# Decoder layer with a product-key mixture of experts: second tile's expert selection moved behind the first one-hots, gates evicted key by key, all second norms closed on VectorE

## The chip, the cores and the metric

The kernel runs on one core of a Trainium2 chip. The metric is the time of one execution on the device in microseconds (us); runs are compared by their medians. Engine names: PE is TensorE (matmuls), DVE is VectorE, ACT is ScalarE, POOL is GpSimd, SP is SyncE, which issues most DMAs.

## The reference

One decoder layer over 512 tokens of width 1024. A token mixer (sliding-window attention beside a gated linear recurrence) is followed by a layer norm, and then by a mixture of 16,384 experts, each a single neuron, chosen by product keys. The part that matters here is that mixture and the norm behind it:

```
q = (ht @ peer_w_q).reshape(T, 8, 2, 128)
s1, s2 = q[:, :, 0] @ keys_1.T, q[:, :, 1] @ keys_2.T
v1, i1 = top_k(s1, 16);  v2, i2 = top_k(s2, 16)
sc, ci = top_k(v1[..., :, None] + v2[..., None, :], 16)
experts = 128 * i1[ci // 16] + i2[ci % 16]
gates = softmax(sc)
out = sum over the 128 experts e of a token:  gate * gelu(h . u[e]) * v[e]
h = layer_norm(ALPHA * h + out)
```

## The kernel before

The 512 tokens are four tiles of 128. Three of them (tiles 1, 2 and 3, in this order) are "dense": the kernel computes the activation of all 16,384 experts for every token and multiplies it by a gate that is zero for an expert not chosen. Tile 0 is done last by gathering the rows of its chosen experts from memory.

After the mixer the work goes through these stages.

- **Queries and scores.** `query(i)` (16 of them, lines 755 to 766) multiplies a block of the query weights with all tokens; `scores(i)` (768 to 777) multiplies the result with the keys, and `top16` (737 to 751) takes, on DVE, the 16 best of 128 keys for each of four tiles.
- **Selection.** `experts(t)` (796 to 870) is a generator that DVE works off in steps for one tile: for each half of the eight heads it adds up candidate scores (`cand`, lines 807 to 813), takes the 16 best (`top16` into `esc` and `pos`), and turns positions into key numbers by comparisons and sums over 128 x 1024 tables (`ge`, `pr`, lines 821 to 847; there is one buffer of each). A step ends at each `yield`; the first half of a head set gives 4 yields, the second 6, and then the softmax and the key numbers `ex` follow.
- **One-hots and gates.** For a dense tile `gate_prep` (878) transposes the key numbers and gates on PE (line 881) and DVE copies them out (`eT`, `gT`, lines 883 and 886). In 48 steps of 8 tokens (16 steps for a tile), `onehots` (898) builds one-hot rows of both key numbers on DVE (lines 910, 917 and 918, with a part on ACT in line 916), and `gate_mm` (923) multiplies them on PE into a PSUM tile `psg` of 8 tokens x 128 keys. That tile is evicted: keys 60 to 127 go to a staging tile `gst` on ACT (line 936) and from there to memory; keys 0 to 59 meet the activations that are kept in `act`: those whose activation is already there are multiplied on DVE (line 939), the rest is copied on ACT (line 941).
- **Activations.** `u_block` (255 to 283) makes the activations of 128 experts for the 384 dense tokens: a 512 KB block of `uT` is loaded, split into two f16 parts on ACT (line 202) and DVE (line 203, `wl`), and multiplied in 24 matmuls of 384 columns. These blocks are what PE does between the gate matmuls.
- **Second matmul and gathers.** From about 605 us PE alternates the remaining `u_block`s with `vblock`s (1051), while DVE and POOL do the gathered tile.
- **Second norm.** `finish(t)` (1140 to 1162) adds the residual, takes the mean and the inverse deviation with `layer_stats` and `rsqrt` on DVE, normalises and stores.

The order on each engine is not written out by hand. The program is recorded in the order of the Python code, and a list scheduler puts each engine's instructions in a static order; `tc.issue_after(last[0].ins)` (line 1003) holds the selection steps behind the newest one-hots. In the loop over queries (981 to 987) the selections of tiles 1 and 2 both advance by one step in each of the four iterations 8 to 11, which covers the first half of the heads of either tile. The rest of tile 1's selection follows in lines 990 to 992, interleaved with `u_block`s; the rest of tile 2's is worked off by `steps(gen, ...)` (line 1004) during tile 1's 16 one-hot steps, two steps each in the first four and one each after that.

In the eviction, `o2` is the PSUM tile as (token, key), `GST[0]` and `W[0]` have the key ahead of the token, and `part` turns the destination, so that the innermost index of both sides is the key: PSUM is read word after word, and `gst` and `act` are read and written with a distance between neighbours (16 and 384 words).

Of the kernel before, what the change touches and what calls it, by code (L numbers as in the profile page):

```python
# [9 lines left out]
F32 = mybir.dt.float32  # L10
# [4 lines left out]
AF = mybir.ActivationFunctionType  # L15
OP = mybir.AluOpType
AX = mybir.AxisListType.X

P = 128
S = 512  # L20
D = 1024
NT = 4
# [22 lines left out]
NW = 60  # L45
# [93 lines left out]
def program(tc, nc, a, out, dbg=None, stop=None):  # L139
    ctx = ExitStack()  # L140
    with ctx:
        _program(ctx, tc, nc, a, out, dbg or {}, stop)


def _program(ctx, tc, nc, a, out, dbg, stop):
    V, A, G, T = nc.vector, nc.scalar, nc.gpsimd, nc.tensor
# [19 lines left out]
    def mk(pool, shape, dt, tag, bufs):  # L166
        uid[0] += 1
        return pool.tile(shape, dt, name=f"{tag}_{uid[0]}", tag=tag, bufs=bufs)
# [58 lines left out]
    def layer_stats(pool, src, tag):  # L227
        st = mk(pool, [P, 2, 6], F32, tag + "st", 2)
        for i in range(2):
            V.bn_stats(st[:, i], src[:, i * 512:(i + 1) * 512])  # L230
        mv = mk(pool, [P, 2], F32, tag + "mv", 2)
        V.bn_aggr(mv, st)
        ve = mk(pool, [P, 1], F32, tag + "ve", 2)
        V.tensor_scalar(ve, mv[:, 1:2], EPS, None, op0=OP.add)
        return mv, rsqrt(pool, ve, tag)
# [3 lines left out]
    def raw4():  # L239
        return mk(rp, [P, 1024], F32, "raw", RAW_BUFS)  # L240
# [383 lines left out]
    for c in range(4):  # L624
        rnn_ssq(c, sqr[c])
    V.tensor_reduce(ssq.rearrange("p t k -> p (t k)"), ssp[:, :8 * NT].rearrange("p (a g) -> p a g", g=4), axis=AX,
                    op=OP.add)
# [11 lines left out]
    for c in range(DC):  # L639
        r = raw4()  # L640
# [69 lines left out]
    pp = ctx.enter_context(tc.tile_pool(name="pp", bufs=1))  # L710
# [44 lines left out]
    def query(i):  # L755
        r = raw4().rearrange("p (c e) -> p c e", c=DC)
        nc.sync.dma_start(r, a["w_q"][i])
        wh, wl = whl()
        split(r, wh, wl, int((i + 1) * Q_POOL) > int(i * Q_POOL))
        o = bank()  # L760
        for sl in (slice(T0, S), slice(0, T0)) if i == 0 else (slice(0, S),):
            for c in range(DC):
                mm3(o[:, sl], wh[:, c], wl[:, c], hh[:, c, sl], hl[:, c, sl], c, c == 0, c == DC - 1)
        qt = mk(gp, [P, S], F32, "k2", K2_BUFS)
        A.activation(qt, o, AF.Copy, scale=1.0 / WS)
        QT[i] = qt

    def scores(i):
        hd, side = divmod(i, 2)
        qt = QT.pop(i)  # L770
        o = bank()
        for t in range(NT):
            T.matmul(o[:, t * P:(t + 1) * P], qt[:, t * P:(t + 1) * P], keys[:, side], start=True, stop=True)
        sc = mk(gp, [P, NT, NKEY], F32, "k2", K2_BUFS)
        A.activation(sc, o.rearrange("p (t k) -> p t k", t=NT), AF.Copy)
        top16([(VV[t][:, hd, side], II[t][:, hd, side], sc[:, t]) for t in TORDER],
              lambda i, src, w=mk(gp, [P, NT, NKEY], F32, "k2", K2_BUFS): w[:, i])
# [7 lines left out]
    first = {}  # L785
# [90 lines left out]
    NB = 8  # L876
# [44 lines left out]
    GST = {}  # L921

    def gate_mm(col0, ob, oh, ol):
        o2 = mk(PB["g"][0], [P, NB, P], F32, "psg", PB["g"][1])
        for t in range(NB):
            q = (slice(None), t // R, slice(None), t % R)
            T.matmul(o2[:, t], ob[q], oh[q], start=True, stop=False)
            T.matmul(o2[:, t], ob[q], ol[q], start=False, stop=True)
        ch, q = divmod(col0, TCH)
        if q == 0:  # L930
            GST[0] = mk(gp, [P, NKEY - NW, TCH], F32, "gst", 2)

        def part(ap):
            return ap.rearrange("p e r -> p r e")

        A.activation(part(GST[0][:, :, q:q + NB]), o2[:, :, NW:], AF.Copy)
        na = min(nact[0], NW)
        wc = W[0][:, :, col0:col0 + NB]
        V.tensor_tensor(part(wc[:, :na]), part(wc[:, :na]), o2[:, :, :na], op=OP.mult)
        if na < NW:  # L940
            A.activation(part(wc[:, na:]), o2[:, :, na:NW], AF.Copy)
        ncol[0] = col0 + NB
        if q == TCH - NB:
            i = max(i for i in range(NQ) if cut[i] <= ch)
            nc.sync.dma_start(gscr[i][:, :, ch - cut[i]].rearrange("g p e t -> p g e t"),
                              GST[0].rearrange("p (g e) t -> p g e t", e=GE))
# [30 lines left out]
    order = TORDER  # L977
# [3 lines left out]
    for i in range(2 * HEADS):  # L981
        query(i)
        if i:
            scores(i - 1)
        if HEADS <= i < HEADS + YH:
            for t in first:
                next(first[t])
    scores(2 * HEADS - 1)
    banks(2, 2)
    while not next(first[order[0]], 1):  # L990
# [8 lines left out]
    for s in range(NS):  # L999
        i, k = divmod(s, SPT)  # L1000
        if k == 0:
            gen = first[order[1]] if i == 0 else experts(order[2]) if i == 1 else iter(())
        with tc.issue_after(last[0].ins):
            steps(gen, 99 if k == SPT - 4 else 2 if k < 4 else 1)
        if k == SPT - 1 and i + 1 < ND:
            gate_prep(order[i + 1])
        nxt = onehots(order[(s + 1) // SPT], (s + 1) % SPT * NB) if s + 1 < NS else None
        if nu[0] < NW - RES:
            u_block()
        gate_mm(s * NB, *pend)  # L1010
        pend = nxt
# [11 lines left out]
    def rows(*offs, scale=None):  # L1023
        rr = []
        for off in offs:
            r = mk(dg[0], [P, D], F32, "gr", GR_BUFS)
            nc.sync.dma_start(r, rowb(off, D))
            if scale is not None:
                A.activation(r, r, AF.Copy, scale=scale)
            rr.append(r)  # L1030
        return rr
# [37 lines left out]
    for b in range(NKEY):  # L1069
# [3 lines left out]
        g, k = divmod(b - NW, GE)  # L1073
# [21 lines left out]
        if b >= NW:  # L1095
            wc = w.rearrange("p (c t) -> p c t", t=TCH)
# [6 lines left out]
        if b == NKEY - NY:  # L1103
            l2g, l2b = rows(R_L2G, R_L2B)
            l1 = rows(R_L1G, R_L1B, scale=ALPHA)
            res = {}
            for t in range(NG, NT):
                y = raw4()
# [31 lines left out]
    def finish(t):  # L1140
        if t < NG:
            y = gacc[t]
            V.tensor_tensor(y, ah[t], gacc[t], op=OP.add)
        else:
            y = res[t]
            for hf in range(2):
                sl = slice(hf * 512, hf * 512 + 512)
                V.scalar_tensor_tensor(y[:, sl], acc[t - NG][hf], 1.0 / GS, y[:, sl], op0=OP.mult, op1=OP.add)
        mv, ri = layer_stats(pp, y, "ln2")
        if t == NT - 1:  # L1150
            for hf in range(2):
                sl = slice(hf * 512, hf * 512 + 512)
                V.scalar_tensor_tensor(y[:, sl], y[:, sl], mv[:, 0:1], l2g[:, sl], op0=OP.subtract, op1=OP.mult)
                V.scalar_tensor_tensor(y[:, sl], y[:, sl], ri, l2b[:, sl], op0=OP.mult, op1=OP.add)
                (nc.sync, nc.scalar)[hf].dma_start(out[t * P:(t + 1) * P, sl], y[:, sl])
            return
        nm = mk(pp, [P, 1], F32, "ln2nm", 2)
        V.scalar_tensor_tensor(nm, mv[:, 0:1], -1.0, ri, op0=OP.mult, op1=OP.mult)
        A.activation(y, y, AF.Identity, scale=ri, bias=nm)
        V.tensor_tensor(y, y, l2g, op=OP.mult)  # L1160
        V.tensor_tensor(y, y, l2b, op=OP.add)
        nc.sync.dma_start(out[t * P:(t + 1) * P], y)

    for t in range(NT - 1):
        finish(t)
    with tc.high_priority():
        finish(NT - 1)
# [15 lines left out]
```

## Time and profile before

| | us |
|---|---|
| median of 3 runs (1374.76 to 1376.82) | 1375.07 |
| the profiled execution, its own time | 1375.56 |
| its span, first to last instruction | 1373.8 |
| PE busy | 1327.5 (97%) |
| DVE busy | 1192.3 (87%) |
| ACT busy | 678.6 (49%) |
| POOL busy | 394.8 (29%) |

The span is shorter than the execution's own time by what lies before the first and behind the last instruction. The shares are averages over stages with different limits, so they have to be read stage by stage; PE's matmuls overlap each other, and a busy PE is not PE at its peak.

### The profile page before, as it was taken

The numbers are of one execution on the slowest core, as the hardware profiler recorded it, in microseconds if no ns is written. First come the engines' busy times: TensorE is split into PE (matmuls) and PEld (weight loads), VectorE is DVE, ScalarE is ACT, GpSimd is POOL, SyncE is SP. The second block draws the span as 40 slices with busy tenths as digits, with TensorE's granted clock in tenths as the row PEclk, the third lists the DMA queues.
The fourth block names the chain that finished last, engine by engine and source line by source line (L and its number), as shares of the span: only waits on it lengthen the run. The fifth ranks groups of instructions, "written<-read, shape, count | busy, mean of one in ns | idle before, by whom it ended". The sixth has DMA issues, their size and how long they took to land.

```text
span 1373.8 us, 21409 instructions
## 1 busy us (share of the span) xinstructions
PE 1327.5 (97%) x7601; PEld 721.3 (53%) x7601; DVE 1192.3 (87%) x2555; ACT 678.6 (49%) x1155; POOL 394.8 (29%) x300
## 2 busy tenths in 40 slices
PE   8999999998999989999999999999999999999996
PEld 3554555554666656655555555555555554444442
DVE  7956766899899998989898888888898889988887
ACT  5755165434798877765433333333333333333341
POOL 0103412300000000000654545445454555545400
PEclk9998999999999999999999999999999999999998
DMA  8103053223465564665999999999999999998851
GB/s 308 64 16 123 3 176 118 93 74 123 129 167 158 145 173 135 167 228 183 394 408 396 356 355 369 364 365 366 367 361 358 351 346 365 354 330 306 305 207 74
DMA packets 142859, 332.49 MB, mean 242 GB/s; under 512 B 62880, under 2 KB 63392, under 8 KB 142752
## 3 DMA queue, kind: packets, MB, share of 16 engines
q1 hardware_dynamic: 105168, 195.59, 42.4%
q0 software_dynamic: 36864, 134.23, 26.4%
q8 instruction: 59, 0.97, 0.3%
q10 hardware_dynamic: 720, 1.31, 0.3%
q14 instruction: 48, 0.39, 0.1%
HBM read 313.53 MB, written 17.56 MB: 241 GB/s over the span
## 4 chain that ended last, share of the span: by engine, by line
PE 76%; DVE 18%; ACT 2%; issue 2%; DMA 2%; POOL 0%; DVEq 0%; SPq 0%; ACTq 0%; POOLq 0%
PE psv L1056 22%; PE psv L1058 11%; PE psu L208 8%; PE psu L206 8%; PE psu L207 8%; PE psv L206 3%; PE psv L207 3%; PE psv L208 3%; DVE wl L203 3%; DVE oab L910 2%; PE psv L475 2%; DVE k L917 1%; PE psv L661 1%; PE psv L662 1%; PE psv L663 1%
## 5 line engine op out<-in xcount | busy, mean ns | idle before, releaser
L715 POOL DMA_INDIRECT gr<-u,ei x128 | 162.7, 1271 | 524.8 <-ACT act L278 369.6
L206 PE MATMUL psu<-hh,wh 128*128 128x384 f16 (+2 forms) x816 | 265.4, 326 | 7.1 <-ACT wh L202 3.0
L208 PE MATMUL psu<-hh,wl 128*128 128x384 f16 (+1 forms) x816 | 265.7, 326 | 5.1 <-DVE wl L203 5.1
L207 PE MATMUL psu<-hl,wh 128*128 128x384 f16 (+1 forms) x816 | 265.6, 326 | 0.0
L202 ACT ACTIVATE wh<-raw 128x1024 f16<-128x1024 f32 (+1 forms) x141 | 147.8, 1048 | 193.7 <-PE psu L207 150.1
L1056 PEld LDWEIGHTS <-w_h 128*128 128x128 f16 x1536 | 150.3, 98 | 173.5
L203 DVE SCALAR_TENSOR_TENSOR wl<-raw,wh 128x1024 f16<-128x1024 f32 (+1 forms) x141 | 171.3, 1215 | 66.1 <-ACT wh L202 65.8
L715 POOL DMA_INDIRECT gr<-v,ei x128 | 170.6, 1333 | 164.7 <-DVE gacc L967 144.4
L1099 ACT ACTIVATE w_h<-act 128x384 f16<-128x384 f32 x128 | 66.1, 521 | 255.7 <-PE psv L1056 254.3
L206 PEld LDWEIGHTS <-wh 128*128 128x128 f16 x1232 | 121.4, 99 | 102.6 <-ACT wh L202 9.4
L1056 PE MATMUL psv<-vl,w_h 128*128 128x512 f16 x582 | 173.4, 379 | 0.0
L1058 PE MATMUL psv<-vh,w_l 128*128 128x512 f16 x582 | 173.4, 379 | 0.0
L208 PEld LDWEIGHTS <-wl 128*128 128x128 f16 x1232 | 121.2, 98 | 99.0 <-DVE wl L203 9.1
L1056 PE MATMUL psv<-vh,w_h 128*128 128x512 f16 x582 | 171.6, 379 | 0.0
L207 PEld LDWEIGHTS <-wh 128*128 128x128 f16 x1232 | 121.4, 99 | 94.3 <-issue 7.9
L967 DVE SCALAR_TENSOR_TENSOR gacc<-gr,gact,gacc 128x1024 f32<-128x1024 f32 x127 | 162.4, 1279 | 0.7
L957 DVE SCALAR_TENSOR_TENSOR gr<-gr,ah 128x1024 f32<-128x1024 f32 x128 | 154.0, 1216 | 1.4 <-DMA gr<-u,ei 1.3
L1094 DVE TENSOR_TENSOR vl<-rv,vh 128x1024 f16<-128x1024 f32 x97 | 118.1, 1218 | 7.6 <-ACT vh L1093 7.6
L1058 PEld LDWEIGHTS <-w_l 128*128 128x128 f16 x768 | 75.1, 98 | 90.6
L208 PE MATMUL psv<-hh,wl 128*128 128x384 f16 (+2 forms) x352 | 119.8, 342 | 1.9 <-DVE wl L203 1.9
L206 PE MATMUL psv<-hh,wh 128*128 128x384 f16 (+2 forms) x352 | 119.8, 342 | 1.5 <-ACT act L278 0.8
L207 PE MATMUL psv<-hl,wh 128*128 128x384 f16 (+2 forms) x352 | 119.9, 342 | 0.0
(264 smaller groups left out, 2050.3 us busy)
## 6 DMA issues: line engine op xcount, KB each, us to landing
raw<-uT SPq DMA_DIRECT2D x128, 512.0 KB, 4.8
rv<-v SPq DMA_DIRECT2D x98, 512.0 KB, 6.8
raw<-v SPq DMA_DIRECT2D x30, 512.0 KB, 7.1
gs<-gst SPq DMA_DIRECT2D x24, 544.0 KB, 4.2
gsb<-gs SPq DMA_DIRECT2D x34, 384.0 KB, 8.5
raw<-w_q SPq DMA_DIRECT2D x16, 512.0 KB, 4.2
raw<-w_in SPq DMA_DIRECT2D x13, 512.0 KB, 4.8
raw<-w_out SPq DMA_DIRECT2D x8, 512.0 KB, 4.3
```

The costliest lines, as they stand in the source:

```text
L202: A.activation(hi, raw, AF.Copy, scale=WS)
L203: V.scalar_tensor_tensor(lo, raw, WS, hi, op0=OP.mult, op1=OP.subtract)
L206: T.matmul(o, lh, rh, start=first, stop=False)
L207: T.matmul(o, lh, rl, start=False, stop=False)
L208: T.matmul(o, ll, rh, start=False, stop=last)
L715: G.indirect_dma_start(out=r, out_offset=None, in_=table, in_offset=bass.IndirectOffsetOnAxis(ap=idx, axis=0))
L957: V.scalar_tensor_tensor(r, r, 1.0 / ALPHA, ah[t], op0=OP.mult, op1=OP.mult, accum_out=gact[t][:, j:j + 1])
L967: V.scalar_tensor_tensor(gacc[t], r, gact[t][:, j:j + 1], gacc[t], op0=OP.mult, op1=OP.add)
L1056: T.matmul(acc[t][hf], w_h[:, tt], vv[:, hf * 512:hf * 512 + 512], start=f and vv is vh, stop=False)
L1058: T.matmul(acc[t][hf], w_l[:, tt], vh[:, hf * 512:hf * 512 + 512], start=False, stop=l)
L1094: vs = V.tensor_tensor(vl, rv, vh, op=OP.subtract)
L1099: A.activation(w_h, w, AF.Copy)
```

## The change

Three edits. (1) In iterations 8 to 11 of the query loop only tile 1's selection advances; tile 2's whole selection is left to the steps inside tile 1's one-hots. (2) In `gate_mm` the PSUM tile is turned instead of the destination: the innermost index is now the token, so that `gst` and `act` are written (and `act` is read) in runs of eight neighbouring words, and neighbours in PSUM are read 128 words apart. (3) `finish` ends in the same way for every tile: per half of 512 columns two `scalar_tensor_tensor` on DVE and a store, the halves on the SP and the ACT queue; the ScalarE normalisation and the two full-width DVE operations of the first three tiles go.

```diff
-        def part(ap):
-            return ap.rearrange("p e r -> p r e")
-
-        A.activation(part(GST[0][:, :, q:q + NB]), o2[:, :, NW:], AF.Copy)
+        ok = o2.rearrange("p t k -> p k t")
+        A.activation(GST[0][:, :, q:q + NB], ok[:, NW:], AF.Copy)
         na = min(nact[0], NW)
         wc = W[0][:, :, col0:col0 + NB]
-        V.tensor_tensor(part(wc[:, :na]), part(wc[:, :na]), o2[:, :, :na], op=OP.mult)
+        V.tensor_tensor(wc[:, :na], wc[:, :na], ok[:, :na], op=OP.mult)
         if na < NW:
-            A.activation(part(wc[:, na:]), o2[:, :, na:NW], AF.Copy)
+            A.activation(wc[:, na:], ok[:, na:NW], AF.Copy)
...
         if HEADS <= i < HEADS + YH:
-            for t in first:
-                next(first[t])
+            next(first[order[0]])
...
         mv, ri = layer_stats(pp, y, "ln2")
-        if t == NT - 1:
-            for hf in range(2):
-                sl = slice(hf * 512, hf * 512 + 512)
-                V.scalar_tensor_tensor(y[:, sl], y[:, sl], mv[:, 0:1], l2g[:, sl], op0=OP.subtract, op1=OP.mult)
-                V.scalar_tensor_tensor(y[:, sl], y[:, sl], ri, l2b[:, sl], op0=OP.mult, op1=OP.add)
-                (nc.sync, nc.scalar)[hf].dma_start(out[t * P:(t + 1) * P, sl], y[:, sl])
-            return
-        nm = mk(pp, [P, 1], F32, "ln2nm", 2)
-        V.scalar_tensor_tensor(nm, mv[:, 0:1], -1.0, ri, op0=OP.mult, op1=OP.mult)
-        A.activation(y, y, AF.Identity, scale=ri, bias=nm)
-        V.tensor_tensor(y, y, l2g, op=OP.mult)
-        V.tensor_tensor(y, y, l2b, op=OP.add)
-        nc.sync.dma_start(out[t * P:(t + 1) * P], y)
+        for hf in range(2):
+            sl = slice(hf * 512, hf * 512 + 512)
+            V.scalar_tensor_tensor(y[:, sl], y[:, sl], mv[:, 0:1], l2g[:, sl], op0=OP.subtract, op1=OP.mult)
+            V.scalar_tensor_tensor(y[:, sl], y[:, sl], ri, l2b[:, sl], op0=OP.mult, op1=OP.add)
+            (nc.sync, nc.scalar)[hf].dma_start(out[t * P:(t + 1) * P, sl], y[:, sl])
```

The scheduler makes a new order of it on PE, DVE, ACT and SP. Three places on DVE are shown.

First, DVE behind the last scores, some 15 us ahead of the first one-hots. Before, `pr_2769` and `es_448` belong to the first half of tile 2, `ge_3209` and `pr_3210` to the second half of tile 1, and `wl` is the low part of a `u_block`'s weights:

```order
L846 TENSOR_TENSOR pr_2769<-ge_2768,bx_2780 128x1024
L857 TENSOR_TENSOR gate_568_3335<-esc_2468,gm_3329 128x128
L828 TENSOR_TENSOR pr_2769<-pr_2769 128x4x128
L834 TENSOR_TENSOR ge_3209<-pj_3207,tabs_1903 128x1024
L203 SCALAR_TENSOR_TENSOR wl_3557<-raw_3554,wh_3556 128x1024
L828 TENSOR_TENSOR pr_2769<-pr_2769 128x4x64
L828 TENSOR_TENSOR pr_2769<-pr_2769 128x4x32
L829 TENSOR_TENSOR es_448_2489<-pr_2769 128x64
L835 TENSOR_TENSOR pr_3210<-ge_3209,tabs_1903 128x1024
```

The same place after the change (`pos_3017`, `ge_3140` and `pr_3141` are the second half of tile 1):

```order
L751 MAX_INDEX pos_3017<-esc_2468,mr_529_3100 128x8
L822 CAST pj_3138<-pos_3017 128x64
L851 TENSOR_TENSOR esc_2468<-esc_2468,gm_3260 128x128
L834 TENSOR_TENSOR ge_3140<-pj_3138,tabs_1903 128x1024
L203 SCALAR_TENSOR_TENSOR wl_3274<-raw_3271,wh_3273 128x1024
L835 TENSOR_TENSOR pr_3141<-ge_3140,tabs_1903 128x1024
```

Tile 2's sums no longer stand between the end of tile 1's candidates and tile 1's second half. From the last common place to the first one-hots there are also 11 `wl` instead of 14: three `u_block`s come later on DVE, and their matmuls come behind the first gate matmuls on PE.

Second, DVE where the one-hots go over from tile 1 to tile 2. Before, the selection of tile 2 was done some steps earlier, and `eT` stands between one-hots of tile 1 (`oab_4360`, `oab_4426`):

```order
L910 TENSOR_TENSOR oab_4360<-iota_1895,eT_3376 128x2048
L939 TENSOR_TENSOR act_1888<-act_1888,psg_4339 128x8x23
L910 TENSOR_TENSOR oab_4426<-iota_1895,eT_3376 128x2048
L883 CAST eT_4496<-psv_4492 128x2x16x8
L886 TENSOR_SCALAR gT_4498<-psv_4492 128x128
```

After the change, `ex`, which the transposes of line 881 wait for, stands just ahead of `eT`, and the first one-hots of tile 2 (`oab_4506`) just behind it:

```order
L829 TENSOR_TENSOR es_573_3361<-pr_3666 128x64
L938 TENSOR_TENSOR act_1888<-act_1888,psg_4471 128x25x8
L867 CAST ex_3895<-es_573_3361 128x128
L938 TENSOR_TENSOR act_1888<-act_1888,psg_4551 128x26x8
L276 TENSOR_TENSOR act_1888<-act_1888,utmp_4547 128x120
L883 CAST eT_4496<-psv_4492 128x2x16x8
L886 TENSOR_SCALAR gT_4498<-psv_4492 128x128
L910 TENSOR_TENSOR oab_4506<-iota_1895,eT_4496 128x2048
```

The selection of tile 2 now fills nearly all of tile 1's steps and ends at the last moment; from tile 2's one-hots on the order is nearly that of before, and in tile 3's it is the same.

Third, DVE at the very end, where the last half of the last tile (`raw_13577`) meets the norm of the third (`raw_13573`). Before:

```order
L1158 SCALAR_TENSOR_TENSOR ln2nm_13823<-ln2mv_13807,ln2y_13811 128x1
L1148 SCALAR_TENSOR_TENSOR raw_13577<-psv_6918,raw_13577 128x512
L1160 TENSOR_TENSOR raw_13573<-raw_13573,gr_13559 128x1024
L230 BN_STATS ln2st_13831<-raw_13577 128x6
L1161 TENSOR_TENSOR raw_13573<-raw_13573,gr_13561 128x1024
L232 BN_AGGR ln2mv_13834<-ln2st_13831 128x2
```

After (line 1151 multiplies by the inverse deviation, 1146 is the old line 1148):

```order
L1151 SCALAR_TENSOR_TENSOR raw_13573<-raw_13573,ln2y_13811,gr_13561 128x512 x2
L1146 SCALAR_TENSOR_TENSOR raw_13577<-psv_6918,raw_13577 128x512
L230 BN_STATS ln2st_13831<-raw_13577 128x6
L232 BN_AGGR ln2mv_13834<-ln2st_13831 128x2
L234 TENSOR_SCALAR ln2ve_13836<-ln2mv_13834 128x1
```

The third tile is finished before the last half is touched, and nothing stands between that half and its statistics.

## Rows read from the trace of the kernel before

**Rows 1.** The page, part 1: busy us, share of the span, instructions.

```profile
PE 1327.5 (97%) x7601; PEld 721.3 (53%) x7601; DVE 1192.3 (87%) x2555; ACT 678.6 (49%) x1155; POOL 394.8 (29%) x300
```

**Rows 2.** Windows by stage: length, busy us (count) of PE, PEld, DVE, ACT, POOL; clock, DMA.

```profile
258.00:345.00 87.00, 76.61 (x435) 43.16 (x433) 86.27 (x492) 37.18 (x52) 6.39 (x3) 1.00 0.30 96
345.00:424.00 79.00, 78.17 (x648) 53.04 (x647) 72.92 (x178) 66.20 (x141) 0.00 (x0) 1.00 0.55 150
424.00:518.00 94.00, 87.57 (x689) 57.24 (x687) 90.80 (x237) 76.87 (x161) 0.00 (x0) 0.98 0.60 160
518.00:592.00 74.00, 69.58 (x579) 46.65 (x580) 71.07 (x97) 57.69 (x142) 0.00 (x0) 0.98 0.57 152
...
605.00:1361.00 756.00, 755.88 (x3896) 380.93 (x3894) 670.27 (x959) 294.07 (x396) 333.31 (x256) 1.00 0.91 335
1361.00:1374.00 13.00, 0.00 (x0) 0.00 (x0) 8.38 (x22) 1.24 (x1) 0.00 (x0) 0.61 0.21 81
```

**Rows 3.** Waits of DVE from 258 to 592 us: total, times, longest.

```profile
DVE eT L883 <- PE psv L881: 4.4, 2, 2.5
DVE wl L203 <- ACT wh L202: 3.2, 3, 1.7
DVE act L939 <- ACT gst L936: 2.2, 5, 0.5
DVE vv L741 <- ACT k L775: 1.6, 1, 1.6
```

**Rows 4.** Waits of PE from 258 to 605 us, the two longest totals.

```profile
PE psu L208 <- DVE wl L203: 5.1, 3, 2.4
PE psg L927 <- DVE k L917: 4.4, 5, 1.3
```

**Rows 5.** Lines: the evictions of `psg`, all together (busy us, mean ns | idle before).

```profile
L936 ACT ACTIVATE gst<-psg 128x544 f32<-128x544 f32 x48 | 50.5, 1127 | 1.6 <-PE psg L928 1.5
L939 DVE TENSOR_TENSOR act<-act,psg 128x88 f32<-128x88 f32 (+47 forms) x48 | 35.1, 735 | 2.2 <-ACT gst L936 2.2
L941 ACT ACTIVATE act<-psg 128x392 f32<-128x392 f32 (+47 forms) x48 | 24.2, 517 | 3.3 <-DVE act L939 3.1
```

**Rows 6.** Lines by form: line 939 in the middle of tiles 3, 2 and 1.

```profile
L939 DVE TENSOR_TENSOR act<-act,psg 128x400 f32<-128x400 f32 x1 | 1.0, 1043 | 0.0
L939 DVE TENSOR_TENSOR act<-act,psg 128x272 f32<-128x272 f32 x1 | 0.7, 710 | 0.0
L939 DVE TENSOR_TENSOR act<-act,psg 128x136 f32<-128x136 f32 x1 | 0.4, 402 | 0.0
```

**Rows 7.** Lines by form: readers of PSUM with contiguous words on both sides.

```profile
L775 ACT ACTIVATE k<-psv 128x512 f32<-128x512 f32 x16 | 9.4, 586 | 0.0
L436 DVE SCALAR_TENSOR_TENSOR z<-psv,rowq 128x512 f32<-128x512 f32 x4 | 2.7, 680 | 0.0
L437 DVE SCALAR_TENSOR_TENSOR z<-psv,rowq 128x256 f32<-128x256 f32 x4 | 1.6, 407 | 0.0
```

**Rows 8.** The chain that ended last, 740 to 760 us: start, length, what.

```profile
742.42 0.86 PE psv L1056 x4
```

**Rows 9.** Windows of tiles `pr` and `esc` on DVE, 258 to 345 us (three half selections).

```profile
258.00:345.00 87.00, 14.95 (x41) 1.00 0.30 96
...
258.00:345.00 87.00, 12.47 (x100) 0.31 (x1) 1.00 0.30 96
```

**Rows 10.** Timeline of the end, DVE and PE: start, length, what [idle before].

```profile
1342.76 1.22 DVE L1094 TENSOR_TENSOR gr<-raw,gr 128x1024 f16<-128x1024 f32 x1 [0.89 <-ACT gr L1093]
1346.25 1.23 DVE L1160 TENSOR_TENSOR gacc<-gacc,gr 128x1024 f32<-128x1024 f32 x1 [1.31 <-ACT gacc L1159]
...
1360.51 0.38 PE L1058 MATMUL psv<-gr,w_l 128*128 128x512 f16 x1
...
1362.81 1.23 DVE L1160 TENSOR_TENSOR raw<-raw,gr 128x1024 f32<-128x1024 f32 x1 [0.70 <-ACT raw L1159]
1365.99 1.40 DVE L1153 SCALAR_TENSOR_TENSOR raw<-raw,ln2mv,gr 128x512 f32<-128x512 f32 x2
```

## The prediction

> **What bounds the kernel now.** The page's shares come first [rows 1]: PE 97%, DVE 87%. They are averages and decide nothing, so the next view is the table of windows, cut near the first one-hots of tiles 1, 2 and 3 [rows 2]. Two stages stand out. From 605 to 1361 us PE is busy for 755.88 of 756 us: there PE sets the pace, and whatever reaches this stage earlier ends earlier by as much. From 258 to 592 us DVE is the engine without holes: 86.27 + 72.92 + 90.80 + 71.07 = 321.1 us busy of 334, so it is idle for 12.9. PE's idle time in the same windows is 10.4, 0.8, 6.4 and 4.4, together 22.1 us. The lists of waits confirm who holds whom. DVE's waits there are few [rows 3]; PE's longest are for DVE, for the split weights of a `u_block` and for one-hots [rows 4]. So between the last queries and the second matmul the time is DVE's work plus some 13 us, and a microsecond taken from DVE there is worth up to one at the end, as long as PE still has idle time to give: at most 22.1 us in all, and next to nothing from 345 to 424, where PE is busy for 78.17 of 79 us.
>
> The end is a stage of its own. PE's last matmul starts at 1360.51 us and lasts 0.38 [rows 10]; what follows is DVE's chain and the last store. 0.2% of the median, 2.75 us, is about what a measurement of this kernel can tell from no change.
>
> **Selection of tile 2, moved.** Half a selection shows in the windows by tile: three halves (tile 1's two and tile 2's first) put 14.95 us on `pr` and 12.47 us on `esc` between 258 and 345 us [rows 9], 5.0 and 4.2 us each; with the comparisons that write `ge` and the candidate sums I estimate 11 to 12 us for a half. Nothing of it is removed. It leaves the stage ahead of the first one-hots and comes back in tile 1's 16 steps. Both belong to the stretch that DVE bounds, so the sum of DVE's work is the same and the term is zero at first order. The first one-hots come earlier by this half, and by the three `wl` that the order moves behind them as well; tile 1's steps then take longer by the same amounts. Two things can spoil that balance. On one side DVE may run dry in the queries, where it depends on PE for scores: the part of the half that ran before the last scores came (its `top16` and candidates, about 5 us) is given back only if DVE was behind. DVE waited for scores (line 741) once after 258 us, 1.6 us at the very start [rows 3], so it was behind from then on: 0 to 5 us, I take 1. On the other side stands the new place of `eT`: DVE waits 4.4 us in two waits for the transposes of line 881 [rows 3], at the starts of tiles 1 and 3, where `ex` stands just ahead of `eT`; tile 2's start had no such wait and now gets that pattern. A third wait of 1.9 to 2.5 us would cost about 2, but at the start of tile 1 a `wl` now stands in the gap, and two short operations stand in the new one: 0 to 2.5 us, I take 0.4. ScalarE's two `bx` copies for the half move along, into a stage where ACT has 66.20 of 79 us [rows 2]; ACT's time is hidden behind DVE.
>
> **Gates evicted key by key.** This is the term that carries the forecast. Today ACT takes 1127 ns for 544 words into `gst`, and DVE 1043, 710 and 402 ns for 400, 272 and 136 words of `act` [rows 5, 6]: about 2.4 ns a word on DVE. Readers of PSUM with neighbouring words on both sides are cheaper [rows 7]: ACT 586 ns for 512, 1.14 ns a word with all that is fixed, so at most 623 for 544; DVE 407 ns for 256 and 680 for 512, 1.07 ns a word over 134 ns, so 561, 425 and 279 ns for the three widths. What makes today's evictions dear is the distance between neighbours in SBUF. The change puts eight words together there and moves the distance to PSUM, and no row shows a PSUM read with a distance. It is bounded below by the contiguous price just worked out. Above, the nearest row is today's strided price, which would leave everything as it is; nothing excludes a dearer one, and that is a rival below. I take the contiguous price, because PSUM has speed to spare: four matmuls of 512 columns go into it in 0.86 us [rows 8], 0.42 ns for a word that is added to what is there, against the 1.14 and 1.07 ns at which ACT and DVE ask. A reader that lost half of that would still not be held up.
>
> [...]
>
> The sum at the contiguous price: DVE saves 123, 285 and 482 ns per step in tiles 1, 2 and 3, over 16 steps each 2.0, 4.6 and 7.7 us. ACT saves 48 x 0.50 = 24 us in line 936 and something in line 941, all off the bound, except that DVE's five waits for `gst`, 2.2 us [rows 3], shorten: I take 1.1. Not all of DVE's part counts. In tile 1 PE is full [rows 2], and it also receives the matmuls of the three moved blocks: 0 of 2.0. In tile 2 PE has 6.4 us to give: 4.6 of 4.6. In tile 3 it has 4.4: I take 3.5 of 7.7; there PE is late next. That makes 4.6 + 3.5 + 1.1 = 9.2 us; ends: 0 with the strided price, 15 if PE's idle time is used up nearly whole.
>
> **Second norm on DVE alone.** For each of the first three tiles two full-width operations go (1.23 us for the one at 1346.25 [rows 10], some 2.4 for both) with one on a single column, and four half-width ones come, two pairs of about 1.4 us like the pair at 1365.99 [rows 10]: DVE gets about 0.3 us more work per tile, 0.9 in all. Against that three idle times go: 1.31 and 0.70 us, in which DVE waits for ACT's normalisation, and 0.89 at 1342.76 ahead of a weight split, which tile 0's first pair now fills [rows 10]. Net -2.0 us; the ends are -2.9, if the extra work hides in other gaps, and +0.9, if DVE then waits for PE instead, whose last result of 1360.9 us nothing here brings forward. The stores of the first three tiles become six halves on two queues; each is issued earlier than the next tile's and nothing is queued behind them on ACT, which has no work left. The last store stays as it is.
>
> **Sum**, against the profiled execution's 1375.56 us: -9.2 + 1 + 0.4 - 2.0 = -9.8, which gives 1365.8. The median of the runs is 0.5 lower than that execution, so 1365.3; I say 1365.
>
> **Rivals.**
>
> 1. *The distance costs in PSUM what it cost in SBUF.* Lines 936, 939 and 941 keep their times, and what is left is +1 + 0.4 - 2.0 = -0.6: 1374.5. [...] Against it: the 0.42 ns of PSUM under matmuls.
> 2. *The distance costs more in PSUM.* This is the case that is slower than before. Line 939 stands 48 times on the engine that bounds the stretch. Rival 1's 0.6 us are eaten when its mean rises from 735 ns by 13; by 70, to 805 ns, the change is slower by over 0.2%: (0.6 + 2.75) / 48. At twice the present price a word, it would be 48 x 0.73 = 35 us on DVE: 1409. Lines 936 and 941 would take another 75 us on ACT, whose 238 us of the 334 [rows 2] would then come near the whole. Against it: the same as against the first.
> 3. *DVE runs dry in the queries.* The eviction is cheap, but about 5 us of the moved half is not given back, since DVE was ahead of the scores after all, and tile 1's steps pay it: 1365 + 4 = 1369. For it: scores come one query at a time, and DVE did wait for them at 258 us [rows 3]. Against it: DVE's 86.27 of 87 us [rows 2].
>
> That the selection is not moved at all can be left out: the order shows it.
>
> **How the numbers follow.** The forecast has 0.61, with a range of its own from 1359 to 1369; rival 1 has 0.18, rival 2 0.11, rival 3 0.10. The range from 1359 to 1375.5 takes in the forecast, rivals 1 and 3, and leaves out rival 2 and the ends. Faster by over 0.2% means under 1372.3: forecast and nearly all of rival 3, 0.70. Within 0.2%: rival 1, 0.18. Slower: rival 2 with a little of rival 1's upper end, 0.12.
>
> **What would show it.** Line 936 near 620 ns and line 939 near 430 in the mean confirm the price; 1127 and 735 are rival 1, more is rival 2. Tile 1's first one-hots should start some 12 to 14 us earlier than before, and tile 2's first at about the time of before; if these come 4 us or more later, rival 3 holds. DVE should show three waits for line 881. PE should be at 100% some 8 us earlier than 605, and the time from PE's last matmul to the end should be about 11 us instead of 13. If the price comes true and PE's idle time before 605 stays at 20 us, the reading that DVE bounds the stretch was wrong.

## The result, and the profile after

The changed kernel takes 1360.7 us (median of 5 runs, 1357.21 to 1362.7) against 1375.42 of the kernel before (5 runs, 1374.76 to 1377.52): a ratio of 0.9881, 95% interval 0.987 to 0.9892. The medians are 14.7 us apart, which would be 0.9893. The ratio is formed from all runs, not from the medians, and makes 16.4 us (14.9 to 17.9). The forecast was 1365.0, 9.8 us less than before, with a range from 1359 to 1375.5. The profiled execution took 1360.70 us, 1358.9 of it span.

The page's first part, which answers to [rows 1]: VectorE has lost 12.2 us of work, ScalarE 26.5.

```profile
PE 1323.5 (97%) x7601; PEld 721.4 (53%) x7601; DVE 1180.1 (87%) x2558; ACT 652.1 (48%) x1152; POOL 395.3 (29%) x300
```

The three evictions after the change, by line (answers to [rows 5]; line, operation, out<-in, count, then busy us, mean ns, and idle time before):

```profile
L935 ACT ACTIVATE gst<-psg 128x544 f32<-128x544 f32 x48 | 29.3, 628 | 4.6 <-PE psg L928 4.5
L938 DVE TENSOR_TENSOR act<-act,psg 128x88 f32<-128x88 f32 (+47 forms) x48 | 20.6, 433 | 0.5 <-ACT gst L935 0.3
L940 ACT ACTIVATE act<-psg 128x392 f32<-128x392 f32 (+47 forms) x48 | 15.3, 324 | 1.3 <-DVE act L938 1.1
```

And by form, for the widths of [rows 6]:

```profile
L938 DVE TENSOR_TENSOR act<-act,psg 128x400 f32<-128x400 f32 x1 | 0.6, 565 | 0.0
L938 DVE TENSOR_TENSOR act<-act,psg 128x272 f32<-128x272 f32 x1 | 0.4, 424 | 0.0
L938 DVE TENSOR_TENSOR act<-act,psg 128x136 f32<-128x136 f32 x1 | 0.3, 285 | 0.0
```

The prediction had 561, 425 and 279 ns, and at most 623 for ScalarE. So a distance of 128 words in PSUM costs VectorE at most 6 ns over the estimate and leaves ScalarE 5 ns above its bound.

The first one-hots of tiles 1, 2 and 3 in VectorE's timeline (start, length, what), of the kernel before:

```profile
351.47 2.35 DVE L910 TENSOR_TENSOR oab<-iota,eT 128x2048 f16<-128x2048 f16 x2
...
423.69 1.22 DVE L910 TENSOR_TENSOR oab<-iota,eT 128x2048 f16<-128x2048 f16 x1
...
517.90 2.35 DVE L910 TENSOR_TENSOR oab<-iota,eT 128x2048 f16<-128x2048 f16 x2
```

and of the changed one:

```profile
338.64 2.35 DVE L910 TENSOR_TENSOR oab<-iota,eT 128x2048 f16<-128x2048 f16 x2
...
420.80 2.35 DVE L910 TENSOR_TENSOR oab<-iota,eT 128x2048 f16<-128x2048 f16 x2
...
510.80 2.35 DVE L910 TENSOR_TENSOR oab<-iota,eT 128x2048 f16<-128x2048 f16 x2
```

Tile 1's come 12.8 us earlier and tile 2's 2.9: tile 1's steps now hold the selection that stood ahead of them.

Windows by stage of the changed kernel (length; busy us and count of PE, PEld, DVE, ACT, POOL; clock, DMA share, GB/s):

```profile
258.00:333.00 75.00, 70.02 (x393) 39.33 (x391) 73.01 (x424) 32.03 (x44) 6.71 (x3) 1.00 0.28 85
333.00:352.00 19.00, 17.34 (x129) 11.37 (x130) 18.66 (x59) 11.44 (x25) 0.00 (x0) 1.00 0.51 155
352.00:424.00 72.00, 72.00 (x591) 48.61 (x590) 70.17 (x195) 57.14 (x134) 0.00 (x0) 1.00 0.60 168
424.00:508.00 84.00, 81.00 (x652) 53.88 (x651) 81.67 (x230) 62.51 (x150) 0.00 (x0) 0.98 0.58 161
508.00:592.00 84.00, 82.33 (x671) 55.05 (x669) 71.66 (x112) 59.50 (x154) 0.00 (x0) 1.00 0.59 166
```

The same cuts of the kernel before, the two that differ most:

```profile
333.00:352.00 19.00, 13.67 (x82) 7.66 (x81) 15.93 (x39) 9.77 (x14) 0.00 (x0) 1.00 0.33 111
...
508.00:592.00 84.00, 78.66 (x628) 51.86 (x629) 78.34 (x116) 62.36 (x147) 0.00 (x0) 0.97 0.58 155
```

From 333 to 352 us, around the first one-hots, both engines had stood still: VectorE for 3.1 us of 19, TensorE for 5.3. Now it is 0.3 and 1.7. In tile 3 TensorE's idle time fell from 5.3 to 1.7 us and its clock column rose from 0.97 to 1.00.

Waits of the changed kernel, VectorE's from 258 to 592 us, then TensorE's from 258 to 605 (total, times, longest):

```profile
DVE wl L203 <- ACT wh L202: 8.2, 5, 2.4
DVE oab L910 <- PE psg L928: 3.5, 4, 1.1
DVE eT L883 <- PE psv L881: 3.3, 2, 1.9
...
PE psu L208 <- DVE wl L203: 3.2, 1, 3.2
PE psu L206 <- ACT act L278: 3.0, 2, 2.5
PE psv L881 <- ACT act L278: 1.9, 1, 1.9
...
PE psg L927 <- DVE k L917: 1.0, 2, 0.6
```

Against [rows 3, 4]: VectorE now waits for TensorE (`oab` for the gate matmuls' buffers; `wl` behind `wh`, and `wh`, by its own waits, for the matmuls of the last `u_block`s), and TensorE's waits for one-hots have gone from 4.4 to 1.0 us. The bound has moved to TensorE in most of the stretch.

The end: TensorE's last matmul, and VectorE's first norm pair behind it; [rows 10] had 1360.51 and 1365.99.

```profile
1347.81 0.38 PE L1056 MATMUL psv<-gr,w_l 128*128 128x512 f16 x1
...
1351.31 1.40 DVE L1150 SCALAR_TENSOR_TENSOR raw<-raw,ln2mv,gr 128x512 f32<-128x512 f32 x2
```

From the last matmul's start to the end 11.1 us are left of 13.3; up to it the changed kernel is 12.7 us ahead.

### The profile page after: what moved, and what is told of

It reads as the page before. It is cut to its first block, busy times and chain, and to the rows that moved or that the text cites. A ratio compares the mean times of both kernels' runs of the same rounds, so it can differ in the third digit from the quotient of the medians.

```text
span 1358.9 us, 21418 instructions
## 1 busy us (share of the span) xinstructions
PE 1323.5 (97%) x7601; PEld 721.4 (53%) x7601; DVE 1180.1 (87%) x2558; ACT 652.1 (48%) x1152; POOL 395.3 (29%) x300
## 4 chain that ended last, share of the span: by engine, by line
PE 81%; DVE 11%; DMA 3%; ACT 1%; issue 1%; POOL 1%; SPq 0%; DVEq 0%; ACTq 0%; POOLq 0%
PE psv L1054 22%; PE psv L1056 11%; PE psu L208 9%; PE psu L207 9%; PE psu L206 9%; PE psv L206 4%; PE psv L208 4%; PE psv L207 4%; PE psg L927 1%; PE psg L928 1%; PE psv L475 1%; DVE wl L203 1%; DMA raw<-w_q 1%; PE psv L432 1%; PE psv L434 1%
```

## The experiments

For every run the time at which TensorE starts its matmuls 1440, 3000, 3690 and the last (7601 in all, counted from 0) is compared with the same start in the trace of before: 287.8, 508.2, 602.3 and 1360.5 us. At the four counts all kernels have done much the same work; the first lies ahead of the first matmul whose place the change moves (at 331 us), and kernels that leave the selection alone are up to 2.4 us late there too, so what differs there (0 to 3.2 us late) is taken as the run's own. "Gain to tile 3" is from the first to the second, "tile 3" from the second to the third, "tail" the shortening of the 13.3 us after the last start. Where the order differs, as in the four kernels from low_to_act on, the cut between these two columns is rough and their sum is not. From 3690 to the last start nothing changes by over 1 us. The ratio is against runs of before on the same chip.

| run | median us | ratio, 95% interval | gain to tile 3 | tile 3 | tail |
|---|---|---|---|---|---|
| the change | 1360.7 | 0.9881 (0.987–0.9892) | 9.1 | 5.0 | 2.2 |
| sel_only | 1374.14 | 0.9984 (0.9974–0.9993) | 4.5 | 1.2 | 0.3 |
| evict_only | 1363.55 | 0.9902 (0.9885–0.9918) | 6.6 | 6.7 | 0.5 |
| norm_only | 1374.06 | 0.9982 (0.9973–0.9992) | −0.4 | 0.5 | 2.5 |
| sel_back | 1362.78 | 0.9899 (0.9882–0.9915) | 6.3 | 6.7 | 2.2 |
| dve_old | 1367.11 | 0.9939 (0.9925–0.9953) | 4.6 | 2.2 | 2.2 |
| act_old | 1361.81 | 0.9902 (0.9888–0.9917) | 9.0 | 4.8 | 2.3 |
| evict_back | 1370.5 | 0.9952 (0.9937–0.9968) | 1.2 | 1.1 | 2.7 |
| runs_of_2 | 1360.79 | 0.9893 (0.9877–0.9909) | 6.2 | 7.7 | 1.8 |
| low_to_act | 1359.95 | 0.9883 (0.9866–0.99) | 8.3 | 7.8 | 2.5 |
| fine_only | 1359.04 | 0.9875 (0.9861–0.9889) | 12.2 | 6.8 | 2.4 |
| fine_steps | 1355.85 | 0.986 (0.9845–0.9875) | 11.2 | 7.4 | 2.4 |
| fine_low | 1353.55 | 0.983 (0.9815–0.9844) | 10.5 | 11.3 | 2.5 |

The stage columns are of one execution each, and two kernels that differ only in the end (sel_only, evict_back) differ by 3.4 us in them; the ratios decide.

**Each part alone, and the change without the first.** The edits are those of the diff.

sel_only:

> The kernel before with the move of the selection alone; evictions and norm as before. Two theories of the 4.9 us by which the whole change gained more than my sum (14.7 against 9.8). Theory S: the move itself gains, because TensorE stood still for 5.8 us between 334 and 346 us just ahead of the first one-hots, and the gate matmuls now come in time to fill that; then this kernel takes 1370 to 1373 us. Theory E: the move is worth what I predicted, between 0 and +1.4 us, and the surplus is the eviction's, in the tile where I counted none of it; then this kernel takes 1375 to 1377 us. In either case its first one-hots start 10 to 13 us earlier than the 351.47 us of before, and the selection's second half stretches tile 1's steps.

evict_only:

> The kernel before with the evictions key by key alone. My sum gave 9.2 us for this: 1366. Theory S (the surplus is the move's): 1366 to 1368. Theory E (the surplus is the eviction's, the 2.0 us of tile 1 and all of tile 3's 7.7 count too): 1361 to 1363. Lines 936, 939 and 941 of before at about 628, 433 and 324 ns in the mean whichever holds.

norm_only:

> The kernel before with the second norm closed by VectorE alone. Sum: 2.0 us, 1373.4, all of it between the last matmul and the end (12.9 us in the trace of before, 10.7 to 11 here), and the last matmul at the same time as before. Rival: the six half stores on two queues and the extra half-width operations take it back, 1375 to 1376.

sel_back, the changed kernel with this undone:

```
         if HEADS <= i < HEADS + YH:
-            next(first[order[0]])
+            for t in first:
+                next(first[t])
```

> The changed kernel with the selection of the second tile again spread over the last four queries; evictions and norm as in the change. Theory S: the gain of the move goes, 1364 to 1367 us against 1360.7. Theory E and my own term (the move costs 0 to 1.4): 1359 to 1361.

Of 1375.5 us the ratios make −2.2 for the selection (1.0 to 3.6), −13.5 for the eviction (11.3 to 15.8) and −2.5 for the norm (1.1 to 3.7). The norm came as the sum had it: all of it in the tail. The eviction carries the change, as forecast, but with more than 9.2. evict_only's median misses theory E's 1361 to 1363 by half a microsecond (by its ratio it would be 1361.9, inside) and theory S's 1366 to 1368 by more. But theory E does not hold alone: the selection's move, which I had costing 1.4 us, gains 2.2 alone (1374.14, between the two theories), and about 2.5 on top of the others (sel_back's 0.9899 against 0.9881; these intervals overlap, and its 1362.78 too lies between the theories). Where it gains shows in the window of sel_only around the first one-hots:

```profile
333.00:352.00 19.00, 18.41 (x135) 12.03 (x136) 18.83 (x58) 12.04 (x28) 0.00 (x0) 1.00 0.47 144
```

TensorE is busy for 18.41 us instead of 13.67 and VectorE for 18.83 instead of 15.93: the move fills the gap ahead of the first one-hots on both.

**The two sides of the eviction.** dve_old and act_old put one side back, evict_back both:

```
dve_old:
-        V.tensor_tensor(wc[:, :na], wc[:, :na], ok[:, :na], op=OP.mult)
+        V.tensor_tensor(part(wc[:, :na]), part(wc[:, :na]), o2[:, :, :na], op=OP.mult)
act_old:
-        A.activation(GST[0][:, :, q:q + NB], ok[:, NW:], AF.Copy)
+        A.activation(part(GST[0][:, :, q:q + NB]), o2[:, :, NW:], AF.Copy)
...
-            A.activation(wc[:, na:], ok[:, na:NW], AF.Copy)
+            A.activation(part(wc[:, na:]), o2[:, :, na:NW], AF.Copy)
```

> The changed kernel with VectorE's product (line 938) alone back in the order of before; ScalarE's two evictions stay key by key. Theory D (VectorE's own work sets the pace between the queries and the second matmul): its 48 products take 35 us again in place of 20.6, and 8 to 13 us come back: 1368 to 1374. Theory A (what helped was ScalarE: the PSUM buffers of the gates and the parked gates come free sooner): 1360 to 1363.

> The changed kernel with ScalarE's two evictions (lines 935 and 940) back in the order of before; VectorE's product stays key by key. Theory D: ScalarE's extra 31 us (48 x 0.50 and 45 x 0.20) hide behind VectorE and only the waits for the parked gates return, 1.1 to 2.2 us: 1361.5 to 1363.5. Theory A: 1368 to 1374.

> The changed kernel with all three evictions of the gates back in the order of before; the selection's move and the norm stay. It closes a square with the changed kernel, dve_old and act_old. If the two sides of the eviction add up, undoing both costs what each costs alone, about 6.5 + 1.5 us: 1368 to 1369. If they hide each other (ScalarE's old evictions delay VectorE and the banks more when VectorE is late too), more is lost, as evict_only's 13 us suggest: 1370 to 1373.

In ratios VectorE's side is worth 8.0 us, ScalarE's 2.9 (its interval touches the change's, so a loss is not certain), both 9.8. Theory D holds, at the low end of the 8 to 13 us that it gave VectorE's side (its 1368 is missed by 0.9), and the sides add up: 10.9 against 9.8. That 1370.5 falls into the range I gave for sides that hide each other is the fault of the range: its 6.5 + 1.5 came from medians beside different runs of before. Why the eviction is worth 13.5 alone and 9.8 here stays open (the two intervals overlap). In dve_old TensorE's largest total of waits is again the one for one-hots (1.0 us in the changed kernel). In act_old waits for ScalarE's eviction appear, which the changed kernel does not have, behind larger ones for line 278:

```profile
PE psg L927 <- DVE k L917: 5.2, 5, 2.0
```

```profile
PE psg L927 <- ACT act L943: 1.9, 3, 1.1
```

So ScalarE's 24 us need not all have been hidden. In the trace of before too TensorE waited for both of its evictions, and in evict_only these two waits are gone:

```profile
PE psg L927 <- ACT gst L936: 2.1, 1, 2.1
...
PE psg L927 <- ACT act L941: 1.1, 1, 1.1
```

**What the price hangs on.** runs_of_2 writes two neighbouring words at a time in SBUF, not eight; PSUM is read at the same distance:

```
+        def pairs(ap):
+            return ap.rearrange("p e (h r) -> p h e r", r=2)
...
+        ok = o2.rearrange("p (h r) k -> p h k r", r=2)
+        A.activation(pairs(GST[0][:, :, q:q + NB]), ok[:, :, NW:], AF.Copy)
```

with lines 938 and 940 in the same manner.

> The changed kernel with the three evictions writing runs of two neighbouring words in SBUF in place of eight; PSUM is read at the same distance of 128 words inside a run. Theory L (each new run costs the writer the same, about 0.9 ns a word for runs of one by lines 936 and 935, so half of that here): line 935 at about 850 to 900 ns, line 938 at about 580 in the mean, 1364 to 1367 us. Theory W (any neighbour is enough): 628 and 433 ns, 1360.7. Theory P (it was PSUM's reading order that cost in before, or runs under 32 bytes are as dear as single words): 1100 and 730 ns, 1368 to 1372.

Its lines:

```profile
L941 DVE TENSOR_TENSOR act<-act,psg 128x88 f32<-128x88 f32 (+47 forms) x48 | 21.4, 445 | 1.8 <-ACT gst L938 1.6
...
L938 ACT ACTIVATE gst<-psg 128x544 f32<-128x544 f32 x48 | 30.4, 637 | 7.1 <-PE psg L928 6.9
```

637 and 445 ns against 628 and 433: theory W. One neighbour gives nearly all of it; the line that copies into `gst` takes 9 ns more, the product 12.

**What is left, and a better version.** low_to_act and the three fine kernels start from the change:

```
low_to_act:
-        na = NB // 2
+        na = 3 * NB // 4
fine_only:
-            fine = h0 or t not in first
+            fine = True
fine_steps, fine_only's edit and:
-            steps(gen, 99 if k == SPT - 4 else 2 if k < 4 else 1)
+            steps(gen, 99 if k == SPT - 4 else 2 if k < 8 else 1)
fine_low, fine_steps's edits and:
-        na = NB // 2
+        na = 3 * NB // 4 if t == TORDER[1] else NB // 2
```

> The changed kernel with six of a step's eight low-half products on ScalarE (line 916) in place of four: VectorE's line 918 shrinks from 512 to 256 words, some 0.13 us a step, 6.4 in all; ScalarE gets 48 x 2 x 0.43 = 41 us more, in stages where it has 64 of 80 us and 65.5 of 90. Theory D still holding after the change: 1357 to 1360. Rival: ScalarE, now close to full, delivers the low halves and the bank evictions late, and TensorE waits: 1362 to 1368.

> The changed kernel with the selection inside the one-hot steps cut finer and begun earlier: the first half of the second tile yields at the same three points as every other half, and steps 4 to 7 of a tile take two pieces instead of one. TensorE's longest stall that is left, 2.55 us at 497.7 behind the last selection pieces of tile 2, and the 4 us at half clock behind it (1.7 us lost) should go: 1356 to 1359. Rival: the stall only moves to another step, 1360 to 1363.

> The changed kernel with only one of fine_steps' two edits: the first half of the second tile yields at the same three points as the others; the number of pieces per step is as in the change. If the finer cut is what removed the stall behind tile 2's last pieces, 1355 to 1357; if the earlier pieces did it, 1360 to 1361.

> fine_steps with six of eight low-half products on ScalarE in tile 2 alone, where low_to_act left TensorE idle for 1.1 us only and cost nothing in ScalarE's waits. TensorE's idle time of fine_steps between 460 and 506, 3.2 us, is what it can give: 1353 to 1355. Rival: the idle time there was not for VectorE's words but for the order: 1356 to 1358.

Moving low halves to ScalarE in all tiles changes nothing that can be told (0.9883). The finer selection alone is within the change's interval (0.9875); with the earlier pieces it is at 0.986, 2.9 us better than the change by ratio, though the intervals still overlap at 0.987 to 0.9875. fine_only's 1359.04 lies between the two ranges given for it, so which of the two edits removes the stall is not settled. With the low halves moved in tile 2 alone it is 0.983, 7.0 us better than the change, clear of its interval: this is the best kernel here. Its windows for tile 2 and for tile 3 with what follows:

```profile
418.00:508.00 90.00, 89.58 (x735) 60.30 (x733) 87.59 (x248) 77.00 (x198) 0.00 (x0) 1.00 0.60 166
508.00:605.00 97.00, 95.56 (x736) 61.41 (x734) 86.77 (x176) 67.08 (x162) 0.00 (x0) 1.00 0.67 199
```

TensorE is idle for 0.4 and 1.4 us, and its clock does not fall in either. The rival to fine_low (that the idle time there came from the order alone) fell with 1353.55.

## Why the prediction was right, and which terms were mis-sized

**What bounds the kernel**: right. The stage of the second matmul has the same length in both traces (from 602.3 and 589.6 us to the last matmul, 758.2 each), so what reached it earlier ended earlier by as much. VectorE set the pace from 258 to 592 us: dve_old takes back 8.0 us with nothing but 14.6 us of its work (line 938 from 20.6 to 35.2 us). TensorE's idle time in these windows fell from 22.1 to 11.3 us, where 20 would have spoken against it.

**Price of the eviction**: right to 6 ns (565, 424, 285 against 561, 425, 279). The reason given for it, that PSUM has speed to spare, is not tested by any run. Rivals 1 and 2 fell: with PSUM read at a distance of 128 words line 935 took 628 ns and line 938 433 in the mean, under the first rival's 1127 and 735.

**How much of it counts**: mis-sized. I took 9.2 us and gave tile 3 "3.5 of 7.7; there PE is late next", because its window showed 4.4 us of idle time. evict_only gains 6.7 in tile 3, and so does sel_back, which has the same order there. Two things were left out of TensorE's time to give. First, the cut at 518 us put idle time of tile 2's end, behind which tile 3 stands, into the window before. Second, busy time at half clock counts as busy: 2.00 us of 2.00 at a clock of 0.50 from 590 to 592 us. The windows of the kernel before show such a stretch (PE's clock in the third column from the end):

```profile
584.00:588.00 4.00, 1.70 (x22) 1.17 (x21) 4.00 (x6) 3.66 (x9) 0.00 (x0) 1.00 0.55 112
588.00:590.00 2.00, 2.00 (x21) 1.41 (x19) 2.00 (x4) 1.60 (x4) 0.00 (x0) 0.76 0.61 234
590.00:592.00 2.00, 2.00 (x7) 0.91 (x6) 2.00 (x3) 0.79 (x5) 0.00 (x0) 0.50 0.81 186
592.00:594.00 2.00, 2.00 (x12) 1.18 (x11) 0.26 (x1) 0.05 (x1) 0.00 (x0) 0.89 1.16 295
```

Ahead of it TensorE's timeline has the longest wait of that stage:

```profile
587.83 0.22 PE L927 MATMUL psg<-k,oab 128*128 128x128 f16 x1 [2.15 <-ACT gst L936]
```

TensorE idles for 2.15 us, and soon behind that the granted clock falls to 0.50. In TensorE's timeline matmuls of 384 columns start 0.32 us apart from 589.13 to 592.33 us, and 0.16 apart from 592.72 on. By the clock column that is (0.24 + 0.50 + 0.11) x 2 = 1.7 us of work lost, as much as about 3.4 us at 0.50 lose. A second stretch of the same length lies between 506 and 512 us (0.50 from 508 to 510); TensorE is busy for 2.85 us of it, so 1.4 lost. Both losses are estimates from the clock column. Both stood in [rows 2] as 0.98 in the clock column of two windows, 0.02 x (94 + 74) = 3.4 us, and I read over them. In evict_only neither fall is there (it has two of its own earlier, 0.98 from 258 to 333 and 0.91 from 333 to 352 us, ahead of what is counted here); its window of that place:

```profile
575.00:585.00 10.00, 9.61 (x81) 6.43 (x80) 7.56 (x13) 7.16 (x20) 0.00 (x0) 1.00 0.80 199
```

The account from 352 us on: TensorE's idle time 11.7 us before (0.83, 5.51 and 5.34 in the windows to 424, 508 and 592), 3.2 in evict_only, so 8.5, and 3.1 of clock: 11.6 of the 13.1 by which its lead grows there (matmuls 1740 to 3690). This is an account and not a test. norm_only has the order of before up to the last norms and only the second of the two falls; it starts 1.75 us late, and in the same windows moved by that TensorE idles for 12.3 us; net of the late start its lead at matmul 3690 is 0.1 us. So there, with one of the two falls gone, TensorE waited longer instead, 12.3 us against 11.7: I count lost clock as room, and no run shows that a fall by itself made the kernel later.

The 1.1 us for ScalarE's side were mis-sized too. They counted VectorE's waits for `gst` alone; TensorE's own two waits for ScalarE's evictions, 2.1 and 1.1 us, were left out, and act_old puts the side at 2.9, with the doubt told above.

**Selection moved**: the sign was wrong. "+1" for VectorE running dry did not come, and rival 3 fell: tile 2's one-hots are 2.9 us earlier, not later. "+0.4" for a wait for line 881 at tile 2's start came in part and was outweighed. That wait is there now:

```profile
420.26 0.42 DVE L883 CAST eT<-psv 128x256 f16<-128x256 f32 x1 [1.33 <-PE psv L881]
```

But the one at tile 1's start, 2.5 us before, is gone; with tile 3's there are two waits as before, and their total fell from 4.4 to 3.3 us [rows 3]. The step that failed is "the term is zero at first order". It is zero for VectorE's work, but [rows 2] showed TensorE idle for 10.4 us in the stage that the block leaves, half of it (5.3 us) just ahead of the first gate matmuls, where VectorE also had its wait of 2.5 us. The gate matmuls now start earlier and fill that. Worth 2.2 to 4.1 us by the runs (sel_only 2.2; evict_back, 6.6, less the norm's 2.5).

**Tile 1, "0 of 2.0"**: nearly right. In evict_only the gain between the first gate matmuls and the end of tile 1 is 0.7 us (matmuls 1740 to 2400); its gain comes in tiles 2 and 3.

**Second norm**: −2.0 forecast, −2.5 measured, 2.2 in the trace. What was said of the tail came true: no second-norm wait for ScalarE is left.

**"What would show it"** said that PE would be at 100% some 8 us before 605. Its lead at matmul 3690 is 12.7 us, 14.1 with the 1.4 by which this run started late: the terms above.

Summed by the runs: 13.5 + 2.2 + 2.5 = 18.2 alone, 16.4 together (14.7 by the medians). Forecast and rivals were told apart rightly; the 61% case came, at the low end of its own range.

## What to carry to other kernels

Before taking an engine's idle time in a stage as the limit of what can be won there, add the time its clock column has lost in that stage (by the account above 3.1 us beside 8.5 of idle time), and look at the idle time just ahead of the cut. A block that moves for nothing on the engine that bounds a stage can still be worth its place: ask what the other engine, idle in the stage that the block leaves, gets to start earlier. When an eviction has to turn a layout, try the distance on the PSUM side with at least two fp32 words together in SBUF: here that took 637 and 445 ns with two words and 628 and 433 with eight, against 1127 and 735 with single words in SBUF and neighbouring ones in PSUM.

## What the runs showed of the hardware that I had not expected

In these evictions two neighbours in SBUF were nearly as good as eight: 637 and 445 ns against 628 and 433, where single words took 1127 and 735 [rows 5]. Why two are enough is not shown by any run. Of the distance in PSUM the two readers show next to no price: at 128 words VectorE took 565, 424 and 285 ns against the contiguous estimate's 561, 425 and 279, and ScalarE 628 against 623.

In the kernel before, TensorE's granted clock fell to 0.50 behind the wait of 2.15 us, and by the estimate above another 1.7 us of work were lost. The changed kernel has one such fall between 500 and 506 us (0.72 in the mean, 0.50 from 502 to 504), behind its wait of 2.5 us for line 278; fine_low, without that wait, has 1.00 from 418 to 508 us. But a wait does not settle it. sel_only has the same wait of 2.15 us at the same matmul, and its clock is 1.00 in the window around it:

```profile
586.62 0.22 PE L927 MATMUL psg<-k,oab 128*128 128x128 f16 x1 [2.15 <-ACT gst L936]
...
584.00:592.00 8.00, 5.85 (x53) 3.95 (x51) 7.06 (x10) 5.41 (x13) 0.00 (x0) 1.00 0.66 180
```

The kernel before waits for 2.2 and 2.9 us between 334 and 345 us with the clock at 1.00, and its fall at 507 us (0.55 from 507 to 508) came behind two stops of under a microsecond each, 0.93 and 0.96 us. No run here settles how much idling it takes.
